# Half rows of 258 + 258 columns become 256 + 260 across a PSUM bank border, with rotating PSUM slots

## The chip, the cores and the metric

The kernel runs on 1 core of one Trainium2 chip. The metric is the device time of that core in microseconds (us). TensorE (PE) does the matrix products, VectorE (DVE) and ScalarE (ACT) the elementwise work, GpSimd (POOL) a little of it, and SyncE (SP) issues the transfers (DMA).

## The reference

One step of a decoder layer for a prompt of 1024 tokens and 8 sample tokens, so 1032 columns, with 1024 channels:

```python
shift, scale, gate = split(silu(c) @ w_ada + b_ada)
h = rms_norm(x, norm_g) * (1 + scale) + shift
(zq, zk, zv, zg_gla, zlr, zb, zc, zh, zg_sc, zx, zg_rg, zm) = split_cols(h @ w_in)
...
o, new_gla = gla_chunked(q, k, v, log_a, s_gla)      # 4 heads
y_gla = (rms_norm(o, gla_ng) * silu(zg_gla)) @ gla_wb
uc, new_sc = causal_dwconv(zc * zh, s_sc, sc_cw)
y_sc = (zb * uc * silu(zg_sc)) @ sc_wb
xc, new_rgc = causal_dwconv(zx, s_rgc, rg_cw)
hr, new_rgh = rg_lru(xc + rg_cb, ...)                # recurrence over tokens
y_rg = (hr * silu(zg_rg)) @ rg_wb
g1, g2, g3 = split(sigmoid(zm + b_merge))
out = (g1 * y_gla + g2 * y_sc + g3 * y_rg) @ w_out
return rms_norm(x + gate * out, final_gain), states
```

## The kernel before

Channels lie on the 128 partitions and tokens on the columns: a row of 1032 columns is two halves of 516 (`HW`). Every fp32 operand of the large products is split into a high and a low part (ACT writes the high part, DVE the rest), and a product is three matmuls: high x high, high x low, low x high. The program goes through four stages.

1. To about 130 us: the rows of x are loaded and normalised, and the modulation is computed from `w_ada`.
2. **The pair stage**, to about 1218 us: `h @ w_in` in 48 pairs of output tiles, in the order of `PAIRS`: for each of the 4 heads `qk`, `v`, `m`, `gg`, then 8 rounds of `rg`, `ch`, `m`, `bs`. A pair is computed with seven products instead of eight, in the order `SEQ = (1, 2, 6, 5, 7, 3, 4)`, from four sums and differences of the operand rows (`b1`, `b2`, `t12`, `t34`). A product is 24 matmuls: 4 slices of the contraction, 3 parts, 2 chunks of 258 columns (`CW`). The products of a pair collect in three PSUM slots: 1, 6, 7, 4 in slot c, 2 in slot b, 5 and 3 in slot d. So c is the first that a pair writes and the last that it leaves. After each product `post` reads the slot: ACT copies it to SBUF (`snap`), or DVE adds it to what was copied.
3. **The branch stage**, to about 1500 us: 24 products `proj`, 3 branches of 8 output tiles, each over 8 slices of the contraction with 3 parts and 3 chunks of 344 columns (`CH`): 72 matmuls. The operands are read back from DRAM (`ul`) and split into `uh` and `ul`. The gate's modulation (`ada_g`) is mixed in.
4. **The last stage**: `@ w_out` for three column ranges, the residual, the final norm.

A slot is a PSUM tile of two banks of 512 columns (`[P, 2, 512]`), and each chunk begins at the first column of its bank, so a half row in PSUM is two pieces of 258. There are three such slots. `slot_n` counts them off, so that each pair uses the same three in the same order: a pair's c lies where the c of the pair before lay. The weights of the pair stage pass through a ring of 3 raw tiles of 1024 columns (`wraw`) and 5 split half tiles (`wspl`). `zctx.close()` gives both pools back at the end of stage 2. Stages 3 and 4 open pools of their own there: `wpool` (2 raw, 3 high, 2 low tiles of 1024 columns) and `mmp` (2 PSUM tiles of three banks).

Independent small work is put between the matmuls: `fill` holds steps, and `tick` runs one after every fourth matmul in program order. A scheduler then sets the final order of each engine's instructions; each engine, and SP's queue of transfers, executes in that order. In a round of the pair stage `RG.steps` (`chunk`, six groups `rgg` of three matmuls, then `rec`) lies inside the `ch` pair.

Of the kernel before, what the change touches and what calls it, by code (L numbers as in the profile page):

```python
# [10 lines left out]
OP = mybir.AluOpType  # L11
# [10 lines left out]
CW = HW // 2  # L22
# [55 lines left out]
def build(tc, a):  # L78
    nc = tc.nc
    from contextlib import ExitStack  # L80
    with ExitStack() as ctx:
# [43 lines left out]
        def c2(t):  # L125
            return t.rearrange("p (c n) -> p c n", c=2)

        def pv(ps):
            return ps[:, :, :CW]

# [74 lines left out]
        def ada_mm(blk, t, ws, i=None, kk=None):  # L205
            pg = ada_st[blk]
            m = 9 if len(ws) == 1 else 20
            for kk in range(2) if kk is None else (kk,):
                k = 2 * t + kk
                for i_ in range(len(ws)) if i is None else (i,):  # L210
                    c = csl if m == 9 else (c20, c20h)[i_]
                    pe.matmul(pg[:m], c[:, k, :], ws[i_][:, kk * 512:(kk + 1) * 512],  # L212
                              start=(k == 0 and i_ == 0), stop=(k == KT - 1 and i_ == len(ws) - 1))
# [80 lines left out]
        def ada_first(blk, t):  # L294
# [3 lines left out]
            with ExitStack() as order:  # L298
# [8 lines left out]
                ada_mm(blk, t, ws)  # L307
# [20 lines left out]
        def group_rstd():  # L328
# [25 lines left out]
        class Pair:  # L354
            def __init__(self, fa, fb, name, use):
                self.fa, self.fb, self.name, self.use = fa, fb, name, use
                self.w = {}
# [20 lines left out]
            def snap(self, ps, name, scale=1.0):  # L378
                s = snap_tile(self.name + name)
                act.activation(c2(s), pv(ps), AF.Copy, scale=scale)  # L380
# [33 lines left out]
        def add_ps(dst, ps, s, scale=None):  # L414
            if scale is None:
                vec.tensor_add(c2(dst), pv(ps), c2(s))
            else:
                vec.scalar_tensor_tensor(c2(dst), pv(ps), scale, c2(s), op0=OP.mult, op1=OP.add)

        def silu_half(dst, src, view):  # L420
            act.activation(view(dst), src, AF.Sigmoid)
            vec.tensor_mul(view(dst), src, view(dst))

        def flat(t):
            return t
# [12 lines left out]
        def lr_mm(ps_of, k, i, start, stop):  # L438
            for n, x in enumerate(hop[i, k % 4]):
                for c in range(2):  # L440
                    pe.matmul(ps_of(c), first["w"][:, k * P:(k + 1) * P], x[:, c * CW:(c + 1) * CW],
# [4 lines left out]
        def first_mm(k):  # L446
            if k == 0:
# [3 lines left out]
                first_ps.append(slot("lr_ps"))  # L451
            lr_mm(lambda c: first_ps[0][:, c, :CW], k, 1, k == 0, False)
            lr_mm(lambda c: first_ps[0][:, c, :CW], k + 4, 2, False, k == 3)
# [20 lines left out]
        class Gates:  # L474
# [24 lines left out]
            def c21(self, ps):  # L499
                act.activation(c2(half(self.gb, 0)), pv(ps), AF.Sigmoid, bias=self.bias(1))  # L500
# [13 lines left out]
        def alpha_input(p0, pg):  # L514
            zst = tmp("zst", F32R)
            gp.memset(zst[64:128].bitcast(F32), 1.0)
            for lo, hi in ((0, 80), (96, 112)):
                act.activation(c2(half(zst, 0))[lo:hi], pv(p0)[lo:hi], AF.Copy)
                for c in range(2):
                    act.activation(c2(half(zst, 1))[lo:hi, c], pg[c][lo:hi, :CW], AF.Copy)  # L520
            vec.tensor_sub(c2(half(zst, 0))[32:64], pv(p0)[32:64], c2(half(zst, 0))[32:64].bitcast(F32))
            for c in range(2):
                o = c2(half(zst, 1))[32:64, c]
                vec.tensor_sub(o, pg[c][32:64, :CW], o.bitcast(F32))
# [6 lines left out]
        class QK:  # L531
# [16 lines left out]
            def c21(self, ps):  # L548
                act.activation(c2(half(self.hd["k"], 0)), pv(ps), AF.Copy)
# [805 lines left out]
```

## Time and profile before

| | before |
|---|---|
| median of 3 runs | 1629.8 us (1626.99 to 1632.26) |
| the profiled execution's own time | 1629.37 us |
| its span from first to last instruction | 1627.6 us |
| mean granted TensorE clock | 0.983 of full speed |
| PE busy | 1542.9 us (95%), 11594 matmuls |
| DVE busy | 1041.9 us (64%) |
| ACT busy | 733.4 us (45%) |

The profile is of one execution. The own time has 1.8 us more than the span, which lies around the first and the last instruction. A matmul's busy time holds its way through the array, and matmuls overlap, so PE is read here by the distance from one start to the next and by its named waits.

### The profile page before, as it was taken

Reading aid. Unit: us, or ns where it says so; the run is one execution under the profiler, and the core shown is the slowest. Engines: PE = TensorE matmul, PEld = TensorE weight load, DVE = VectorE, ACT = ScalarE, POOL = GpSimd, SP = SyncE. Lnnn points to the kernel's source line nnn. Section 1 sums busy time; section 2 is a strip of 40 time slices with the busy share of each in tenths; the row PEclk is TensorE's granted clock in tenths of the full one; section 3 lists DMA queues with packets and bytes.
Section 4 is the critical chain, followed back from the end, with each engine's and each line's share of the span. In section 5 each row is a group of like instructions: output and inputs, shape, how many; then the busy total and the mean of one; then the engine's idle time right before and its main releaser. Section 6 shows DMA issues by size and latency. Waiting matters only on the chain.

```text
span 1627.6 us, 27671 instructions
## 1 busy us (share of the span) xinstructions
PE 1542.9 (95%) x11594; PEld 1494.1 (92%) x11594; DVE 1041.9 (64%) x1673; ACT 733.4 (45%) x1163; POOL 31.6 (2%) x27
## 2 busy tenths in 40 slices
PE   4899999999999899999999999999997999999996
PEld 3489999999999899999999999999996999999996
DVE  7877587695877957666677667585755343434543
ACT  5556365473565645464444535454543221111332
POOL 3000000000000000000000000000000000000011
PEclk8799999999999999999999999999998999999998
DMA  9011412223232131212121211213135576661423
GB/s 361 16 62 41 146 53 107 79 79 134 78 104 82 66 121 40 91 57 95 66 94 57 78 66 69 92 40 107 41 132 195 207 274 237 218 208 53 143 79 92
DMA packets 58139, 177.45 MB, mean 109 GB/s; under 512 B 7166, under 2 KB 17822, under 8 KB 58014
## 3 DMA queue, kind: packets, MB, share of 16 engines
q1 hardware_dynamic: 58014, 175.68, 30.8%
q8 instruction: 91, 1.49, 0.4%
q14 instruction: 34, 0.28, 0.1%
HBM read 132.64 MB, written 43.02 MB: 108 GB/s over the span
## 4 chain that ended last, share of the span: by engine, by line
PE 49%; ACT 6%; DVE 5%; issue 3%; POOL 1%; DMA 1%; POOLq 0%; SPq 0%; DVEq 0%; ACTq 0%
PE y_ps L1108 17%; PE bs_c L347 6%; PE m_c L347 5%; PE rg_c L347 5%; PE bs_d L347 3%; PE m_d L347 2%; PE rg_d L347 2%; PE ch_c L347 2%; PE bs_b L347 1%; PE rg_b L347 1%; PE wo_ps L1210 1%; PE wo_pg L1210 1%; DVE a L936 1%; PE ch_b L347 1%; PE rgg L914 1%
## 5 line engine op out<-in xcount | busy, mean ns | idle before, releaser
L1108 PE MATMUL y_ps<-uh,y_h 128*128 128x344 f32 x576 | 124.1, 323 | 12.7 <-ACT y_h L164 12.7
L1108 PE MATMUL y_ps<-uh,y_l 128*128 128x344 f32 x576 | 124.5, 322 | 1.9 <-DVE y_l L165 1.9
L1108 PE MATMUL y_ps<-ul,y_h 128*128 128x344 f32 x576 | 124.1, 322 | 0.0
L1108 PEld LDWEIGHTS y_ps<-uh,y_h 128*128 128x128 f32 x576 | 97.6, 190 | 13.3 <-ACT y_h L164 12.9
L1158 DVE TENSOR_TENSOR gl<-y_ps,gl 128x1032 f32<-128x1032 f32 x24 | 29.6, 1232 | 117.4 <-PE y_ps L1108 117.2
L1108 PEld LDWEIGHTS y_ps<-uh,y_l 128*128 128x128 f32 x576 | 97.7, 190 | 4.6 <-DVE y_l L165 4.0
L1108 PEld LDWEIGHTS y_ps<-ul,y_h 128*128 128x128 f32 x576 | 97.9, 190 | 0.9
L164 ACT ACTIVATE y_h<-y_r 128x1024 fp32r<-128x1024 f32 x24 | 25.5, 1062 | 129.6 <-PE y_ps L1108 99.6
L1237 POOL TENSOR_TENSOR yt<-yt,frs 128x776 f32<-128x776 f32 x8 | 14.6, 1856 | 1515.5 <-DVE frs L1234 1515.5
L164 ACT ACTIVATE uh<-ul 128x1032 fp32r<-128x1032 f32 x24 | 25.1, 1062 | 35.5 <-DMA ul<-us 35.5
L165 DVE TENSOR_TENSOR ul<-ul,uh 128x1032 fp32r<-128x1032 f32 x24 | 29.1, 1227 | 17.5 <-ACT uh L164 17.4
L165 DVE TENSOR_TENSOR y_l<-y_r,y_h 128x1024 fp32r<-128x1024 f32 x24 | 29.2, 1216 | 15.0 <-PE ada L212 12.6
L1210 PE MATMUL wo_ps<-mlo,wo_h 128*128 128x388 f32 (+1 forms) x96 | 31.3, 326 | 0.0
L1210 PE MATMUL wo_ps<-mhi,wo_h 128*128 128x388 f32 (+1 forms) x96 | 30.9, 322 | 0.2 <-DVE yt L1217 0.2
L863 DVE SCALAR_TENSOR_TENSOR xc<-xp,pk,xc 128x1022 f32<-128x1022 f32 (+2 forms) x24 | 30.7, 1278 | 0.3
L1210 PE MATMUL wo_pg<-mlo,wo_h 128*128 128x388 f32 (+1 forms) x96 | 30.7, 320 | 0.0
L1210 PE MATMUL wo_ps<-mhi,wo_l 128*128 128x388 f32 (+1 forms) x96 | 30.7, 319 | 0.0
L1210 PE MATMUL wo_pg<-mhi,wo_l 128*128 128x388 f32 (+1 forms) x96 | 30.7, 319 | 0.0
L1210 PE MATMUL wo_pg<-mhi,wo_h 128*128 128x388 f32 (+1 forms) x96 | 30.6, 319 | 0.0
L1227 ACT ACTIVATE fsq<-yt 128x388 f32<-128x388 f32 (+1 forms) x21 | 10.2, 489 | 44.0 <-DVE yt L1222 28.4
L708 ACT ACTIVATE vt<-po 128x128 f32<-128x128 f32 x64 | 14.2, 276 | 33.2 <-PE po L706 33.2
L711 DVE SCALAR_TENSOR_TENSOR S<-S,eB,po 128x256 f32<-128x256 f32 x28 | 13.4, 478 | 23.0 <-ACT vt L708 22.8
(2826 smaller groups left out, 5198.6 us busy)
## 6 DMA issues: line engine op xcount, KB each, us to landing
ul<-us SPq DMA_DIRECT2D x24, 516.0 KB, 6.1
gl<-gs SPq DMA_DIRECT2D x24, 516.0 KB, 6.2
y_r<-wb SPq DMA_DIRECT2D x24, 512.0 KB, 4.1
pps<-gl SPq DMA_DIRECT2D x16, 516.0 KB, 3.5
p<-pps SPq DMA_DIRECT2D x16, 516.0 KB, 5.7
wada<-w_ada SPq DMA_DIRECT2D x16, 512.0 KB, 10.2
gs<-ga SPq DMA_DIRECT2D x12, 516.0 KB, 2.6
gs<-gb SPq DMA_DIRECT2D x12, 516.0 KB, 2.6
```

The costliest lines, as they stand in the source:

```text
L164: act.activation(hi, raw, AF.Copy)
L165: vec.tensor_sub(lo, raw, hi.bitcast(F32))
L347: pe.matmul(ps[:, c, :CW], m[:, k * P:(k + 1) * P], x[:, c * CW:(c + 1) * CW], start=(first and k == 0 and n == 0), stop=(last and k == 3 ...
L708: act.activation(hd["o"][d][:, gcols(g)], po[:, d * P:(d + 1) * P], AF.Copy)
L711: vec.scalar_tensor_tensor(Sn, S, s["eB"][:, gl:gl + 1], po[:, DV:2 * DV], op0=OP.mult, op1=OP.add)
L863: vec.scalar_tensor_tensor(hv(out)[:, :, s:TH], hv(src)[:, :, :TH - s], w(i), hv(out)[:, :, s:TH], op0=OP.mult, op1=OP.add)
L914: pe.matmul(ps, m[:, ws], x[:, cs], start=(ii == 0), stop=(ii == 2))
L936: vec.tensor_tensor_scan(a2[:, ts], aa[:, ts], a2[:, ts], a2[:, TH - 1:TH] if i else 0.0, op0=OP.mult, op1=OP.add)
L1108: pe.matmul(ps[:, c, :CH], m[:, ks], x[:, c * CH:(c + 1) * CH], start=(k == 0 and i == 0), stop=(k == KT - 1 and i == 2))
L1158: vec.tensor_mul(v3(g), psv(ps), v3(g))
L1210: pe.matmul(own(o), m[:, ks], view(x), start=(k == 0 and i == 0), stop=(k == KT - 1 and i == 2))
L1237: (gp if ci < 2 else vec).tensor_mul(y, y, rst_[:, :w].unsqueeze(1).to_broadcast([P, 2, w]))
```

## The change

The two chunks of a half row become 256 and 260 columns. A slot is one tile of 1024 columns; the chunks lie in its columns 256 to 512 and 512 to 772, so they meet at the bank border, and ACT and DVE read a half row as one run of 516 columns. A pair with number n takes c in slot n, b in slot n + 1 and d in slot n + 2 (modulo 3): its c lies where the pair before had b, its b where that had d, its d where that had c. The pools of the pair stage stay open. `proj` becomes a generator that does one half row after the other, 48 matmuls into one slot each, with DVE's multiplication after each half. Its weights and those of the last stage pass through the pair stage's ring, in halves of 512 columns, and the last stage uses the three slots in turn.

```diff
-CW = HW // 2
-        zctx = ExitStack()
-        wz_pool = zctx.enter_context(tc.tile_pool(name="wz_pool", bufs=2))
-        slot_pool = zctx.enter_context(tc.tile_pool(name="slot_pool", bufs=1, space=bass.MemoryType.PSUM))
+        wz_pool = ctx.enter_context(tc.tile_pool(name="wz_pool", bufs=2))
+        slot_pool = ctx.enter_context(tc.tile_pool(name="slot_pool", bufs=1, space=bass.MemoryType.PSUM))
...
-        slot_n = [0]
-
-        def slot(name):
-            i = slot_n[0] % 3
-            slot_n[0] += 1
-            return slot_pool.tile([P, 2, 512], F32, name=name, tag=f"slot{i}", bufs=1)
+        def slot(name, i):
+            return slot_pool.tile([P, 1024], F32, name=name, tag=f"slot{i % 3}", bufs=1)
...
-        def pv(ps):
-            return ps[:, :, :CW]
+        CHUNKS = ((0, 256), (256, HW))
+
+        def pv(ps, c=None):
+            a0, b0 = CHUNKS[c] if c is not None else (0, HW)
+            return ps[:, 256 + a0:256 + b0]
...
                     for c in range(2):
-                        pe.matmul(ps[:, c, :CW], m[:, k * P:(k + 1) * P], x[:, c * CW:(c + 1) * CW],
+                        pe.matmul(pv(ps, c), m[:, k * P:(k + 1) * P], x[:, slice(*CHUNKS[c])],
...
                 if i == 1:
-                    self.c = slot(self.name + "_c")
+                    self.c = slot(self.name + "_c", self.n)
                 elif i == 2:
-                    self.b = slot(self.name + "_b")
+                    self.b = slot(self.name + "_b", self.n + 1)
                 elif i == 5:
-                    self.d = slot(self.name + "_d")
+                    self.d = slot(self.name + "_d", self.n + 2)
...
-        zctx.close()
-        wpool = ctx.enter_context(tc.tile_pool(name="wpool", bufs=2))
-        mmp = ctx.enter_context(tc.tile_pool(name="mmp", bufs=2, space=bass.MemoryType.PSUM))
...
         def load_w(src, name, tag=None):
-            raw = wpool.tile([P, 1024], F32, name=name + "_r", tag="wraw", bufs=2)
+            raw = wraw(name)
             sp.dma_start(raw, src)
...
+            w = [wspl(f"{name}_{i}") for i in range(2)]
+            for i in range(2):
+                split(raw[:, i * 512:(i + 1) * 512], *w[i])
+            return [[w[i][x] for i in range(2)] for x in range(2)]
 
         def proj(src, xhi, xlo, name):
-            whi, wlo = load_w(src, name)
-            ps = mmt(name + "_ps")
-            for k in range(KT):
-                ks = slice(k * P, (k + 1) * P)
-                for i, (m, x) in enumerate(((whi, xhi[k]), (whi, xlo[k]), (wlo, xhi[k]))):
-                    for c in range(NC3):
-                        pe.matmul(ps[:, c, :CH], m[:, ks], x[:, c * CH:(c + 1) * CH],
-                                  start=(k == 0 and i == 0), stop=(k == KT - 1 and i == 2))
-                        tick()
-            return ps
+            w = load_w(src, name)
+            for h in range(2):
+                ps = next_slot(name + "_ps")
+                for k in range(KT):
+                    whi, wlo = (x[k // 4][:, k % 4 * P:(k % 4 + 1) * P] for x in w)
+                    for i, (m, x) in enumerate(((whi, xhi[k]), (whi, xlo[k]), (wlo, xhi[k]))):
+                        for c in range(2):
+                            pe.matmul(pv(ps, c), m, half(x, h)[:, slice(*CHUNKS[c])],
+                                      start=(k == 0 and i == 0), stop=(k == KT - 1 and i == 2))
+                            tick()
+                yield h, pv(ps)
...
-                ps = proj(a["wb"][br, j], [t[0] for t in u], [t[1] for t in u], f"y{br}_{j}")
                 g = tmp("gl")
                 sp.dma_start(g, gs[br][j])
-                vec.tensor_mul(v3(g), psv(ps), v3(g))
+                for h, y in proj(a["wb"][br, j], [t[0] for t in u], [t[1] for t in u], f"y{br}_{j}"):
+                    vec.tensor_mul(half(g, h), y, half(g, h))
...
-                ps = gpt("wo_pg") if f % 2 else mmt("wo_ps")[:, 0]
+                ps = next_slot("wo_ps")
```

The scheduler's order changes with it. The first place is PE's stream where the `m` pair of the second round (`m5`, after `ch1`) begins. Before, `m5` has done product 2 in b and begun product 5 in d when product 1 comes in c, with a wait for DVE:

```order
L347 MATMUL m_b<-b2h_597,m5w_l 128x258 x2
L347 MATMUL m_d<-t12h_356,m5w_h 128x258 [waits DVE_49,Activation_49]
L347 MATMUL m_d<-t12h_356,m5w_h 128x258
L347 MATMUL m_d<-t12l_357,m5w_h 128x258 x2
L347 MATMUL m_c<-b1h_348,m5w_h 128x258 [waits DVE_49]
L347 MATMUL m_c<-b1h_348,m5w_h 128x258
L347 MATMUL m_c<-b1l_349,m5w_h 128x258 x2
```

Now products 1 (24 matmuls in c) and 2 (24 in b) stand ahead, product 6 follows in c, and product 5 is the first to write d:

```order
L342 MATMUL m_b<-b2h_597,m5w_l 128x260
L342 MATMUL m_c<-t12h_356,m5w_h 128x256 [waits Activation_49]
L342 MATMUL m_c<-t12h_356,m5w_h 128x260
...
L342 MATMUL m_c<-t12h_601,m5w_l 128x256
L342 MATMUL m_c<-t12h_601,m5w_l 128x260
L342 MATMUL m_d<-t12h_356,m5w_h 128x256 [waits DVE_49]
L342 MATMUL m_d<-t12h_356,m5w_h 128x260
```

The wait for DVE's read of the `ch` pair's c moved from the pair's first product in c to product 5, 72 matmuls into the pair.

The second place is PE's stream at the end of the pair stage. Before, the first product `y_0` of the branch stage waits for all transfer queues, DVE and ACT at once, with `uh` and `ul` the two parts of its operand rows:

```order
L347 MATMUL bs_c<-t34h_605,bs7w_l 128x258 x2
L1108 MATMUL y_0_ps<-uh_0_13438,y_0_h 128x344 [waits DMAHW3_49,DMAHW4_49,DMAHW2_49,DMAHW5_49,DMAHW1_49,DMAHW6_49,DMAHW0_49,DMAHW7_49,DVE_49,Activation_49]
L1108 MATMUL y_0_ps<-uh_0_13438,y_0_h 128x344 x2
L1108 MATMUL y_0_ps<-ul_0_13439,y_0_h 128x344 x3
L1108 MATMUL y_0_ps<-uh_0_13438,y_0_l 128x344 [waits DVE_49]
```

Now matmuls of the gate's modulation (`ada`) follow the last pair at once, and `y_0` takes its operand rows one by one, each with a wait of its own:

```order
L342 MATMUL bs_c<-t34h_605,bs7w_l 128x260
L207 MATMUL ada<-ada_0_0_h,c_94 20x512
L207 MATMUL ada<-ada_0_0_l,c20h 20x512 [waits DVE_49]
L1098 MATMUL y_0_ps<-uh_0_13430,y_0_0_h 128x256 [waits PE_49,Activation_49]
L1098 MATMUL y_0_ps<-uh_0_13430,y_0_0_h 128x260
...
L1098 MATMUL y_0_ps<-uh_1_13436,y_0_0_h 128x256 [waits Activation_49]
...
L1098 MATMUL y_0_ps<-ul_1_13437,y_0_0_h 128x256 [waits DVE_49]
```

In SP's queue the weights of `y_0` (`y_0_r`) stood behind the last result of the pair stage (`zb`) before:

```order
L483 DMA gs_114<-gb 128x1032
L1145 DMA ul<-us_109 128x1032 x6
L998 DMA us_111<-zb 128x1032
L1145 DMA ul<-us_109 128x1032 x2
L1092 DMA y_0_r<-wb 128x1024
L1092 DMA ada_0_r<-w_ada 128x1024
```

They now stand ahead of it, and of the last two gates:

```order
L1079 DMA y_0_r<-wb 128x1024
L475 DMA gs_114<-ga 128x1032
L475 DMA gs_114<-gb 128x1032
L1079 DMA ada_0_r<-w_ada 128x1024
L1079 DMA ada_1_r<-w_ada 128x1024
L1079 DMA y_1_r<-wb 128x1024
L1135 DMA ul<-us_109 128x1032 x6
L991 DMA us_111<-zb 128x1032
```

The first weights of the branch stage moved from behind the pair stage's last transfer to ahead of its last pair's results.

## Rows read from the trace of the kernel before

**Rows 1.** The page: busy time by engine.

```profile
PE 1542.9 (95%) x11594; PEld 1494.1 (92%) x11594; DVE 1041.9 (64%) x1673; ACT 733.4 (45%) x1163; POOL 31.6 (2%) x27
```

**Rows 2.** Windows: stretch, length, busy time and instructions by engine, granted clock, DMA.

```profile
300.00:400.00 100.00, 100.00 (x833) 98.62 (x833) 74.76 (x129) 56.97 (x109) 0.00 (x0) 1.00 0.27 97
...
1400.00:1440.00 40.00, 40.00 (x256) 40.00 (x255) 12.46 (x11) 4.14 (x4) 0.00 (x0) 1.00 0.78 269
```

**Rows 3.** PE's waits: for whom, us in total, times, longest.

```profile
PE y_ps L1108 <- ACT y_h L164: 12.7, 1, 12.7
PE m_c L347 <- DVE ch L967: 11.1, 8, 1.5
...
PE ch_c L347 <- ACT ch1u L380: 1.2, 1, 1.2
...
PE m_c L347 <- ACT m4u L380: 1.0, 1, 1.0
```

**Rows 4.** Timeline, PE alone: starts in four stretches without other matmuls between.

```profile
1206.70 0.40 PE L347 MATMUL bs_d<-t12h,bs7w_h 128*128 128x258 f32 x2
...
1215.40 0.40 PE L347 MATMUL bs_c<-t34h,bs7w_h 128*128 128x258 f32 x2
...
1460.28 0.63 PE L1108 MATMUL y_ps<-ul,y_h 128*128 128x344 f32 x3
...
1469.73 0.48 PE L1108 MATMUL y_ps<-uh,y_h 128*128 128x344 f32 x2
...
1529.85 0.34 PE L1210 MATMUL wo_ps<-mhi,wo_h 128*128 128x388 f32 x1
...
1533.56 0.34 PE L1210 MATMUL wo_pg<-mhi,wo_h 128*128 128x388 f32 x1
...
1599.76 0.28 PE L1210 MATMUL wo_pg<-mlo,wo_h 128*128 128x256 f32 x1
...
1607.35 0.28 PE L1210 MATMUL wo_pg<-mhi,wo_l 128*128 128x256 f32 x1
```

**Rows 5.** Timeline of the second round's `ch` pair, all engines.

```profile
629.02 0.32 PE L914 MATMUL rgg<-xch,rgwl 128*128 128x344 f32 x1
...
629.94 1.28 ACT L926 ACT_TABLE_LOAD   x1
...
635.24 0.51 PE L347 MATMUL ch_c<-t34h,ch1w_h 128*128 128x258 f32 x2 [1.21 <-ACT ch1u L380]
```

**Rows 6.** Timeline where the `m` pair follows it.

```profile
644.40 0.40 PE L347 MATMUL ch_c<-t34h,ch1w_l 128*128 128x258 f32 x2
...
648.34 0.68 DVE L967 TENSOR_TENSOR ch<-ch_c,cc 128x516 f32<-128x516 f32 x1
...
649.08 0.51 PE L347 MATMUL m_c<-b1h,m5w_h 128*128 128x258 f32 x2 [1.51 <-DVE ch L967]
```

**Rows 7.** Timeline and windows at the end of the pair stage.

```profile
1218.05 0.40 PE L347 MATMUL bs_c<-t34h,bs7w_l 128*128 128x258 f32 x2
...
1218.99 4.86 ACT L164 ACTIVATE uh<-ul 128x1032 fp32r<-128x1032 f32 x5
...
1222.37 4.66 DVE L165 TENSOR_TENSOR ul<-ul,uh 128x1032 fp32r<-128x1032 f32 x4
...
1224.21 0.42 SPq L1092 DMA_DIRECT2D y_r<-wb  x1
...
1230.05 1.06 ACT L164 ACTIVATE y_h<-y_r 128x1024 fp32r<-128x1024 f32 x1 [0.22 <-DMA y_r<-wb]
...
1231.16 1.23 PE L1108 MATMUL y_ps<-uh,y_h 128*128 128x344 f32 x3 [12.71 <-ACT y_h L164]
...
1245.37 0.63 PE L1108 MATMUL y_ps<-uh,y_h 128*128 128x344 f32 x3
...
1218.40:1231.16 12.76, 0.05 (x1) 0.00 (x0) 10.44 (x11) 8.54 (x9) 0.00 (x0) 0.71 0.62 229
1231.16:1236.49 5.33, 5.33 (x19) 5.33 (x19) 3.66 (x3) 2.67 (x3) 0.00 (x0) 0.50 0.80 283
```

More of the change, by code (lines that the diff above doesn't have):

```diff
@@ L306, in ada_first @@
                     split(raw, *ws)
-                ada_mm(blk, t, ws)
+                ada_mm(blk, t, [(w[:, :512], w[:, 512:]) for w in ws])
         def ada_end(blk):
@@ L333, in group_rstd @@
             for s in range(2):
-                ps = slot("rs_ps")
+                ps = slot("rs_ps", s + 1)
                 for g in range(4):
-                    rs["p"] = pe.matmul(ps[:, g // 2, g % 2 * W8:(g % 2 + 1) * W8],
+                    rs["p"] = pe.matmul(ps[:, 512 + (g - 2) * W8:512 + (g - 1) * W8],
                                         rs["sk"][:, (4 * s + g) * P:(4 * s + g + 1) * P], r, start=True, stop=True).ins
-                act.activation(c2(half(rstd, s)), pv(ps), AF.Copy)
+                act.activation(half(rstd, s), ps[:, 512 - 2 * W8:512 + 2 * W8], AF.Copy)
         def product(ps, w, i, ks=range(4), first=True, last=True):
@@ L440, in lr_mm @@
                 for c in range(2):
-                    pe.matmul(ps_of(c), first["w"][:, k * P:(k + 1) * P], x[:, c * CW:(c + 1) * CW],
+                    pe.matmul(ps_of(c), first["w"][:, k * P:(k + 1) * P], x[:, slice(*CHUNKS[c])],
                               start=(start and n == 0), stop=(stop and n == 1))
@@ L548, in c21 @@
             def c21(self, ps):
-                act.activation(c2(half(self.hd["k"], 0)), pv(ps), AF.Copy)
+                act.activation(half(self.hd["k"], 0), pv(ps), AF.Copy)
         def alpha_steps(h):
@@ L639, in c21 @@
             def c21(self, ps):
-                act.activation(c2(half(self.hd["vt"][1], 0)), pv(ps), AF.Copy)
+                act.activation(half(self.hd["vt"][1], 0), pv(ps), AF.Copy)
         def v_steps(h):
@@ L966, in c21 @@
                 n, ch = self.n, self.ch
-                vec.tensor_mul(c2(half(ch, 0)), pv(ps), c2(half(self.cc, 0)))
+                vec.tensor_mul(half(ch, 0), pv(ps), half(self.cc, 0))
                 def cw(i):
@@ L1006, in build @@
             f, cls = where[kind]
-            pairs.append(Pair(*f(n), f"{kind}{n}", cls(n)))
+            pairs.append(Pair(len(pairs), *f(n), f"{kind}{n}", cls(n)))
         masks()
@@ L1074, in build, with next_slot @@
             sp.dma_start(a[name], t)
-        zctx.close()
-        wpool = ctx.enter_context(tc.tile_pool(name="wpool", bufs=2))
-        mmp = ctx.enter_context(tc.tile_pool(name="mmp", bufs=2, space=bass.MemoryType.PSUM))
-        def v3(t):
-            return t.rearrange("p (c n) -> p c n", c=NC3)
-        def psv(ps):
-            return ps[:, :, :CH]
-        def mmt(name):
-            return mmp.tile([P, NC3, 512], F32, name=name, tag="mm", bufs=2)
+        slot_n = [len(pairs)]
+        def next_slot(name):
+            slot_n[0] += 1
+            return slot(name, slot_n[0] - 1)
@@ L1090, in load_w @@
         def load_w(src, name, tag=None):
-            raw = wpool.tile([P, 1024], F32, name=name + "_r", tag="wraw", bufs=2)
+            raw = wraw(name)
             sp.dma_start(raw, src)
             if tag:
-                hi, lo = (bt(tag, name + x, F32R)[:, :1024] for x in ("_h", "_l"))
-            else:
-                hi = wpool.tile([P, 1024], F32R, name=name + "_h", tag="whi", bufs=3)
-                lo = wpool.tile([P, 1024], F32R, name=name + "_l", tag="wlo", bufs=2)
-            split(raw, hi, lo)
@@ L1099, in load_w @@
[L1099 to L1111 removed]
+                w = [bt(tag, name + x, F32R)[:, :1024] for x in ("_h", "_l")]
@@ new lines, in load_w @@
+                split(raw, *w)
+                return [[t[:, i * 512:(i + 1) * 512] for i in range(2)] for t in w]
+            w = [wspl(f"{name}_{i}") for i in range(2)]
+            for i in range(2):
+                split(raw[:, i * 512:(i + 1) * 512], *w[i])
+            return [[w[i][x] for i in range(2)] for x in range(2)]
+        def proj(src, xhi, xlo, name):
+            w = load_w(src, name)
[9 more added lines that the diff above has]
+                yield h, pv(ps)
@@ L1203, in build @@
             for f in range(8):
-                ps = gpt("wo_pg") if f % 2 else mmt("wo_ps")[:, 0]
+                ps = next_slot("wo_ps")
                 o = ps[:, :w]
-                whi, wlo = wo[f]
                 for k in range(KT):
-                    ks = slice(k * P, (k + 1) * P)
+                    whi, wlo = (x[k // 4][:, k % 4 * P:(k % 4 + 1) * P] for x in wo[f])
                     for i, (m, x) in enumerate(((whi, mhi[k]), (whi, mlo[k]), (wlo, mhi[k]))):
-                        pe.matmul(own(o), m[:, ks], view(x), start=(k == 0 and i == 0), stop=(k == KT - 1 and i == 2))
+                        pe.matmul(own(o), m, view(x), start=(k == 0 and i == 0), stop=(k == KT - 1 and i == 2))
                 if f % 2 == 0:
```

60 lines of the change are left out of this document (28 added, 32 removed).

## Prediction

> **What bounds the kernel now.** I read the page first: PE is busy for 95% of the span, DVE for 64% and ACT for 45% [rows 1]. So the time is PE's: the matmuls at their rate, plus the stretches in which PE waits. A window in the heads' part of the pair stage shows PE without a gap at full clock [rows 2]; there only a cheaper matmul can help. PE's waits come next [rows 3]. From the pair stage on, three kinds count: 12.7 us once, ahead of the first product of the branch stage; 11.1 us in 8 pieces, where an `m` pair needs slot c, from which DVE still reads the `ch` pair; and 1.2 us in each of 7 rounds (the row of `ch1u` stands for them), where the seventh product of a `ch` pair needs ACT's copy of the sixth. The first round has a few odd ones, the longest 1.0 us. The waits of the first 130 us belong to loading and normalising, which the change leaves alone. Third I read the distance between matmul starts, since 8064 matmuls of 258 columns make up the pair stage and 1728 of 344 the branch stage.
>
> **What a matmul costs.** Four stretches have nothing else between [rows 4]. Of 258 columns, 72 matmuls start in 8.70 us: 120.8 ns each. Of 344 columns, 60 (20 rows of 3) in 9.45 us: 157.5 ns. Of 388 columns, 21 in 3.71 us: 176.7 ns. Of 256 columns (two runs of 128), 64 in 7.59 us: 118.6 ns. The line through 256 and 344 rises by 0.442 ns a column, and gives 176.9 for 388, as measured. For 258 it gives 119.5, but 120.8 is measured, 1.3 ns more. The forms on the line read operand rows from a column that is a multiple of 4 (16 bytes). Of the two 258s the second starts at column 258, 8 bytes beside such a place. The new chunks start at 0, 256, 516 and 772, all multiples of 4. If that is the reason, two chunks cost 118.6 + 120.4 = 239.0 ns in place of 241.6, and the 4032 chunk pairs of the pair stage save 10.5 us. If the reason is another one, they save 0, since 516 columns stay 516 columns; no row lets me expect a loss. I take the alignment, because three forms lie on one line and the only one off it is the one that starts askew. I book 9 us of the 10.5, as in part of each `ch` pair PE follows ACT and not its own rate.
>
> Here the Trainium skill would say otherwise. Its page "TensorE: Matmul & The Clock Gate", section "Back-to-back issue gap", gives columns divided by 2.4 plus 2.5 ns at full clock, whatever the address; this makes, as an estimate, 110.0 ns for 258 columns, and 220.0 for the two chunks before and after alike. The trace's 120.8 lies above it; whether addresses play a part, no run here shows yet. By the rule the chunks would bring nothing.
>
> **The branch stage.** A product was 72 matmuls at 157.5, 11.34 us; now it is 96, or 48 chunk pairs at 239.0, 11.47 us. For the 23 products after the first that is 3.0 us more; at 241.6 it would be 5.9. I take 3. More DVE instructions (two multiplications of half rows, weights split in halves) lie under PE's work: the window 1400 to 1440 has DVE busy for 12.5 of 40 us [rows 2].
>
> **The `m` waits.** In round 2 the last matmuls of the `ch` pair's c start at 644.40, DVE's read begins at 648.34 and takes 0.68, and the `m` pair starts at 649.08 after 1.51 us of idling [rows 6]. DVE is thus some 4.4 us late. Before, PE bridged part of it with products 2 and 5. Now the new c is the old b, long read, and the first to write the old c is product 5. Ahead of it stand 72 matmuls of the pair, of which 6 come earlier than the last `ch` product: 66 at 119.5 ns cover 7.9 us. So the 11.1 us go. What is late next: DVE must after its read do about two full rows, two taps of full rows and the weights of product 5 before it splits those of product 7. At 0.68 us a half row [rows 6] and 1.17 a full one [rows 7] they are ready at about the time when PE gets there; I expect at most a few tenths of a us. The new b is the old d, whose read has product 4 and the new product 1, 48 matmuls or 5.7 us, to hide in.
>
> **The `ch` waits.** These stay. Between the end of the fourth `rgg` group (629.02) and PE's going on (635.24) lie 6.2 us of ACT: table loads, an exponential, two sigmoids, the copy [rows 5]. In PE's order 31 pair matmuls and 6 of `rgg` stood in between, 4.7 us; now 33 and 6 do, 4.9 us, and two fewer stand ahead of that group. That is 0.45 us a round, 3 us in seven rounds, not the 8.4 of the waits. Of the first round's odd waits I book 1 us.
>
> **The end of the pair stage.** PE's last pair matmul ends about 1218.4. The weights of `y_0` are issued only at 1224.21, split at 1230.05, and PE starts at 1231.16; the clock granted is 0.71 of full speed while PE idles and 0.50 in the 5.3 us after it [rows 7], the lower of its two levels, 1.2 GHz. The next product starts at 1245.37. So `y_0` takes 27.0 us, of which its matmuls need 11.3. Now no pool is closed, its weights are loaded and split before the last pair ends, and PE takes each operand row as it comes. DVE sets the pace. It has seven `ul` at 1.17 us [rows 7], one full row and one half for the last pair's result, and four halves of weights, at 0.68 each: 8.2 + 1.2 + 0.7 + 2.7 = 12.8 us, and about 2 us for ACT's part ahead of it. `y_0` should end some 15.5 us after the last pair, and PE will have done in that time 7 of the modulation's matmuls (1.6 us at 0.23 for 512 columns, by the line above) and about 12 of `y_1` (1.4 us). That saves 27.0 - 15.5 + 3.0 = 14.5 us. PE has little to do in the first 5 us, and the clock may fall again; 5.3 us at half speed would cost 2.65 us. I take 13, with bounds of 10 and 14.5.
>
> **The sum.** 11.1 + 3 + 1 + 9 + 13 - 3 = 34.1 us. The profiled execution's own time is 1629.4, its span 1627.6, its place in the middle of the runs (median 1629.8): 1629.4 - 34.1 = 1595.3, forecast 1595 us. Every addition to ACT, DVE and SP is booked at nothing, since PE is the engine that all others wait for. If DVE's cover were gone, the 48 half-row multiplications (0.68 for half of 1.2) would add some 4 us in the branch stage.
>
> **Rivals.**
> - *Only the columns count* (chance 0.24). For it: the excess is only 1.3 ns, and the 258s are the only form with two chunks. Against it: three widths on one line. The 9 us fall away and the branch stage costs 2.9 more: 1595 + 12 = 1607. The rule of the Trainium skill's page "TensorE: Matmul & The Clock Gate", above, gives this for the chunks.
> - *The gap moves into the splits* (0.10). DVE or the transfers (three weight tiles now go ahead of the six `ul`) come later than I add up, and the clock stays at 0.5 for longer; half of the 13 us is lost: 1601.
> - *The `m` wait comes back at product 7's weights* (0.07). Against it stands my sum of DVE's work, for it that it comes out even. Half of 11.1 us back: 1601.
> - *Slower: the branch stage waits for transfers* (0.03). Its DMA engines are busy for 0.78 at 269 GB/s while PE has no gap [rows 2], and SP issues in one order, in which a transfer that waits for a ring tile holds up all behind it. If PE lost more than 1.7 us in each of 23 products, 39 us, the kernel would be slower by over 0.3%; at 2 us it gives 1641. Against it: the ring has three raw tiles where `wpool` had two, and five half tiles where it had two full low ones, so the next weights are ahead by more.
>
> **How the numbers follow.** The forecast has 0.56. What a measurement can tell from no change is about 0.3%, 5 us. Faster takes the forecast and the first three rivals, less a little for mishaps that I have not seen: 0.93. Same: 0.04, a milder form of the last rival. Slower: 0.03. The range goes from 1583 (the full 10.5 and 14.5 us, and small waits that I have not booked) to 1608 (the first rival), and leaves out some 2 in 10.
>
> **What would show it.** PE's list of waits without `m_c <- DVE ch` and without `y_ps <- ACT`; `ch_c <- ACT` still there at about 1.0 in each of 7 rounds. Two chunks in 239 ns where no other matmul lies between; at 241 to 242 the first rival holds. `y_0` finished about 15 us after the last pair, and in the branch stage 48 chunk pairs in 11.5 us without waits. The forecast is wrong if PE waits at new places: product 5 or 7 of `m`, `ul` rows of `y_0`, or weights of the branch stage.

## The result and the profile after

| | before | after |
|---|---|---|
| median | 1630.3 us (1626.99 to 1632.26, 4 runs) | 1590.7 us (1590.05 to 1592.04, 4 runs) |
| the profiled execution's own time, span | 1629.37, 1627.6 us | 1590.05, 1588.2 us |
| forecast | | 1595 us (1583 to 1608) |

The ratio is 0.976, with an interval of 0.9743 to 0.9778: 39.6 us faster, where 34.1 had been worked out. The sum came out close, but several of its terms were off, in both directions. PE is now busy for 96% of the span (1524.0 us), with 12170 matmuls, 576 more than in [rows 1].

PE's list of waits of after, as [rows 3] (for whom, us in total, times, longest):

```profile
PE wo_ps L1199 <- DVE yt L1206: 3.5, 1, 3.5
...
PE m_d L342 <- DVE m4w_l L160: 2.7, 1, 2.7
...
PE rgg L907 <- ACT xch L159: 2.2, 8, 0.4
...
PE ch_c L342 <- ACT ch3u L375: 0.9, 1, 0.9
```

The two long rows of [rows 3], `y_ps <- ACT` and `m_c <- DVE ch`, are gone. `ch_c` stays, as forecast, at 0.8 to 0.9 in each of 7 rounds. Three rows of those shown are new or larger than before: `wo_ps` in the last stage, `m_d` in the first round, and `rgg`, eight times 0.3 on average. In the first head a wait of 1.7 us for DVE's `vs` is new as well.

Where the time came from is read by cutting both spans at the same places: at the end of the last pair, at the start of the eighth product of the branch stage (`y_7`), and at the start of the last stage. Windows of before, then of after (stretch, length, busy time and instructions of PE, PEld, DVE, ACT, POOL, granted clock, DMA share, GB/s):

```profile
1218.29:1327.78 109.49, 94.91 (x554) 87.83 (x553) 45.30 (x43) 35.05 (x36) 0.00 (x0) 0.94 0.58 208
1327.78:1520.73 192.95, 192.95 (x1227) 192.95 (x1225) 77.67 (x66) 34.74 (x33) 0.00 (x0) 1.00 0.54 187
1520.73:1627.55 106.82, 93.52 (x584) 91.59 (x582) 48.97 (x93) 34.34 (x58) 14.61 (x8) 0.95 0.32 100
```

```profile
1189.80:1282.39 92.59, 92.09 (x722) 88.01 (x720) 48.98 (x65) 35.01 (x49) 0.00 (x0) 1.00 0.74 273
1282.39:1476.63 194.24, 194.24 (x1635) 194.24 (x1634) 82.45 (x100) 38.72 (x51) 0.00 (x0) 1.00 0.51 172
1476.63:1588.16 111.53, 95.25 (x584) 93.11 (x582) 46.29 (x91) 33.60 (x57) 14.61 (x8) 0.94 0.29 91
```

Up to the end of the pair stage 1218.29 - 1189.80 = 28.5 us are won, in the next stretch 109.49 - 92.59 = 16.9; the 17 products that follow cost 1.3 more, the last stage 4.7 more. 28.5 + 16.9 - 1.3 - 4.7 = 39.4, the difference of the spans.

In the pair stage one round shows the pattern. PE's timeline, the first matmul of `rg5`, `ch5`, `m9`, `bs5` and `rg6`, of before and then of after:

```profile
952.61 0.28 PE L347 MATMUL rg_b<-b2h,rg5w_h 128*128 128x258 f32 x1
973.25 0.28 PE L347 MATMUL ch_b<-b2h,ch5w_h 128*128 128x258 f32 x1
995.50 0.28 PE L347 MATMUL m_b<-b2h,m9w_h 128*128 128x258 f32 x1
1020.58 0.28 PE L347 MATMUL bs_b<-b2h,bs5w_h 128*128 128x258 f32 x1
1041.13 0.28 PE L347 MATMUL rg_b<-b2h,rg6w_h 128*128 128x258 f32 x1
```

```profile
935.16 0.28 PE L342 MATMUL rg_c<-b1h,rg5w_h 128*128 128x256 f32 x1
955.16 0.28 PE L342 MATMUL ch_c<-b1h,ch5w_h 128*128 128x256 f32 x1
977.20 0.28 PE L342 MATMUL m_c<-b1h,m9w_h 128*128 128x256 f32 x1
1000.06 0.28 PE L342 MATMUL bs_c<-b1h,bs5w_h 128*128 128x256 f32 x1
1020.06 0.28 PE L342 MATMUL rg_c<-b1h,rg6w_h 128*128 128x256 f32 x1
```

The round goes from 88.52 to 84.90 us: `rg` wins 0.64, `ch` 0.21, `m` 2.22, `bs` 0.55. The terms of the sum for such a round were 1.4 for `m`, 0.45 for `ch`, and 0.75 for the chunks (9 us times 336 of 4032 pairs of chunks), 2.6 in all. So there is more in it than its named waits and the chunks, and `ch` gave least. (By the first starts the last product of `ch` is counted with `m`, in both kernels alike.)

### The profile page after: what moved, and what is told of

It reads as the page before. It is cut to its first block, busy times and chain, and to the rows that moved or that the text cites. A ratio compares the mean times of both kernels' runs of the same rounds, so it can differ in the third digit from the quotient of the medians.

```text
span 1588.2 us, 29025 instructions
## 1 busy us (share of the span) xinstructions
PE 1524.0 (96%) x12170; PEld 1485.4 (94%) x12170; DVE 1048.2 (66%) x1731; ACT 738.4 (46%) x1197; POOL 31.6 (2%) x27
## 4 chain that ended last, share of the span: by engine, by line
PE 73%; DVE 14%; issue 5%; ACT 5%; DMA 1%; POOL 1%; POOLq 0%; DVEq 0%; ACTq 0%; SPq 0%
PE y_ps L1098 17%; PE m_c L342 8%; PE bs_c L342 6%; PE m_d L342 4%; PE rg_c L342 3%; PE ch_c L342 3%; PE gg_c L342 3%; PE qk_c L342 3%; PE bs_d L342 3%; PE wo_ps L1199 3%; DVE xc L856 2%; PE qk_d L342 2%; PE ada L207 2%; PE rg_d L342 1%; PE m_b L342 1%
## 5 line engine op out<-in xcount | busy, mean ns | idle before, releaser
L1098 PE MATMUL y_ps<-ul,y_h 128*128 128x256 f32 (+1 forms) x768 | 153.8, 282 | 0.5 <-DVE ul L160 0.5
L1098 PE MATMUL y_ps<-uh,y_l 128*128 128x256 f32 (+1 forms) x768 | 153.9, 282 | 0.0
L1098 PE MATMUL y_ps<-uh,y_h 128*128 128x256 f32 (+1 forms) x768 | 153.7, 282 | 0.0
L1148 DVE TENSOR_TENSOR gl<-y_ps,gl 128x516 f32<-128x516 f32 x48 | 33.2, 694 | 65.7 <-PE y_ps L1098 64.7
L160 DVE TENSOR_TENSOR y_l<-y_r,y_h 128x512 fp32r<-128x512 f32 x48 | 32.9, 688 | 48.0 <-ACT y_h L159 43.9
L1199 PE MATMUL wo_ps<-mlo,wo_h 128*128 128x388 f32 (+1 forms) x192 | 62.7, 327 | 0.3 <-DVE mlo L160 0.3
L1199 PE MATMUL wo_ps<-mhi,wo_l 128*128 128x388 f32 (+1 forms) x192 | 62.0, 323 | 0.0
L1199 PEld LDWEIGHTS wo_ps<-mhi,wo_h 128*128 128x128 f32 x192 | 36.8, 192 | 3.9 <-DVE yt L1206 3.7
L1199 PEld LDWEIGHTS wo_ps<-mlo,wo_h 128*128 128x128 f32 x192 | 36.9, 192 | 0.9 <-DVE mlo L160 0.6
L1199 PEld LDWEIGHTS wo_ps<-mhi,wo_l 128*128 128x128 f32 x192 | 36.8, 192 | 0.3
```

The lines of the kernel that those rows point to most:

```text
L160: vec.tensor_sub(lo, raw, hi.bitcast(F32))
L1098: pe.matmul(pv(ps, c), m, half(x, h)[:, slice(*CHUNKS[c])], start=(k == 0 and i == 0), stop=(k == KT - 1 and i == 2))
L1148: vec.tensor_mul(half(g, h), y, half(g, h))
L1199: pe.matmul(own(o), m, view(x), start=(k == 0 and i == 0), stop=(k == KT - 1 and i == 2))
```

## The experiments

**The slots alone, and all but the slots.** `rotation_only` is the kernel before with the turned slots and nothing else; `slots_fixed` is the kernel after without them:

```
rotation_only:
-        slot_n = [0]
-
-        def slot(name):
-            i = slot_n[0] % 3
-            slot_n[0] += 1
-            return slot_pool.tile([P, 2, 512], F32, name=name, tag=f"slot{i}", bufs=1)
+        def slot(name, i):
+            return slot_pool.tile([P, 2, 512], F32, name=name, tag=f"slot{i % 3}", bufs=1)
...
-                    self.c = slot(self.name + "_c")
+                    self.c = slot(self.name + "_c", self.n)
slots_fixed:
-            pairs.append(Pair(len(pairs), *f(n), f"{kind}{n}", cls(n)))
+            pairs.append(Pair(0, *f(n), f"{kind}{n}", cls(n)))
```

> The kernel before with one part of the change alone: the slots are turned by one from pair to pair; chunks of 258 in a bank each and the old later stages stay. Theory (the parts add up): the m waits go, 11 us, and with the prediction's small terms 15 us, about 1615 us; with the pauses below 0.2 us in most other pairs (0.37 us in rg7) up to 1608. The ch waits stay at 0.8 to 1.2 us. Rival (DVE's lateness turns up one or two products later, at product 5 or at the weights of product 7): a wait of about 1 us in each m pair at a new place, 1626 to 1630 us.

> The changed kernel, but every pair takes slots 0, 1 and 2 as c, b and d again, so that product 1 of a pair writes the slot which the pair ahead still has to be read from. Theory (the slots are worth what the waits of the kernel before show): PE waits again for DVE's read of the ch pair at each m pair, 8 times about 1.4 us, 11 us; with the 4 us that the prediction booked for the ch waits and the first round this gives 15 us, about 1606 us. The trace of before also has pauses too short for the list of waits, some 0.1 us each where PE goes over to a product in c (0.37 us in the pair rg7, which the changed kernel does not have); if those are the slots' too, there are up to 47 such pairs and the time is nearer 1612. Rival (the waits went because of the chunks or the tail, not the turning): no m wait, 1591 us.

Measured: `rotation_only` 1612.6 us against 1628.0 of before on the same chip, ratio 0.9903 (0.9881 to 0.9925): 15.4 us. `slots_fixed` 1605.5, 14.7 us above the changed kernel. Both times lie in what the theory gave. In `slots_fixed` the waits of `m` for DVE's read come back with 6.7 us, less than the 11.1 of before; the rest lies in longer `ch` waits (1.3 a round) and in short pauses. In `rotation_only` no wait of `m` turned up at a new place in the rounds 2 to 8, so its rival falls. The same round of `rotation_only`:

```profile
943.62 0.28 PE L343 MATMUL rg_c<-b1h,rg5w_h 128*128 128x258 f32 x1
963.92 0.28 PE L343 MATMUL ch_c<-b1h,ch5w_h 128*128 128x258 f32 x1
985.96 0.28 PE L343 MATMUL m_c<-b1h,m9w_h 128*128 128x258 f32 x1
1009.14 0.28 PE L343 MATMUL bs_c<-b1h,bs5w_h 128*128 128x258 f32 x1
1029.45 0.28 PE L343 MATMUL rg_c<-b1h,rg6w_h 128*128 128x258 f32 x1
```

It takes 85.83 us, 2.69 less than before: `m` 1.90, and `rg`, `bs` and `ch` 0.34, 0.24 and 0.21, of which the list of waits had shown nothing for `rg` and `bs`. What such a pause is made of stands in the timeline of before: at the start of `rg7`, DVE reads slot c of `bs6`, and PE goes over to c a moment after.

```profile
1130.98 0.69 DVE L422 TENSOR_TENSOR sz<-bs_c,sz 128x516 f32<-128x516 f32 x1
...
1131.79 0.30 PEld L347 LDWEIGHTS rg_c<-b1h,rg7w_h 128*128 128x128 f32 x2 [0.15 <-issue]
```

DVE's read ends at 1131.67. The pause of 0.15 us before PE's weight load is put down to "issue" and is in no row of PE's list; `slots_fixed` has such pauses by name, `ch_c <- DVE sz`, 7 times, 0.2 us at most.

**The old tail.** The changed kernel's pair stage with the later stages of before (the diff is that of the change from the closing of the pools on, turned round).

> The changed kernel's pair stage, but the stages behind it as they were before: pools closed, three chunks of 344, weights in a pool of their own, five PSUM buffers in the last stage. Theory (the gap at the end of the pair stage belongs to the pools that are closed there): the wait of some 12.7 us for the weights of y_0 and the half clock behind it are back. By the prediction's terms 13 - 3 = 10 us more, 1601; by the places of the same products in both traces 15.6 us more until the last stage, which then runs some 5 us faster than now, so again about 10 to 11 us, 1601 us. Rival (the gap was the lateness of DVE and ACT in the old pair stage, which the turned slots have cured): less than 4 us of it come back, 1588 to 1592 us.

Measured: 1599.0 us, 8.3 above the changed kernel (by the ratios to before, 0.9825 and 0.976, 10.6). PE waits 12.8 us for `y_h` again, although the turned slots are there; the rival falls. `tail_old` and `rotation_only` (1612.6) ran in one session and differ only by the chunks of the pair stage, their cut and their place in PSUM: these are worth 13.6 us there.

**Five buffers in the last stage.** Before, this stage had four PSUM buffers, two large and two small ones (not five, as the expectations say); after the change it has three. Here it gets five.

```
-                ps = next_slot("wo_ps")
+                ps = gpt("wo_pg") if f % 2 else next_slot("wo_ps")
```

> The changed kernel with five PSUM buffers in the last stage again (the three slots for even products, the two small ones for odd), as the kernel before had them by another pool. Theory (with three slots PE runs into DVE in the third piece of the last stage): the new wait of 3.5 us goes and the matmuls around it close up, 3.5 to 5 us less than the changed kernel, about 1586 us. Rival (DVE itself ends last there): PE waits less, the end comes no sooner, 1590 us.

Measured: 1587.3 us (1582.5 to 1589.8), ratio to before 0.974 (0.9722 to 0.9758); against the 0.976 of the change alone the two intervals overlap. In the trace the wait for `yt` is gone, and the last stage takes 106.6 us, against 111.5 of after and 106.8 of before. The rows of after show what it was: DVE waits for a transfer of `x` at 1564.07, and with three slots PE has no place to go on to. Right behind the wait, from 1564.60 to 1568.30, the granted clock is 0.54 on average (its lower level, 1.2 GHz, for most of the time), which by that share costs another 1.7 us. The timeline, and the window of that stretch:

```profile
1564.07 0.89 DVE L1206 SCALAR_TENSOR_TENSOR yt<-wo_ps,modG,yt 128x256 f32<-128x256 f32 x2 [3.32 <-DMA yt<-x]
...
1564.61 0.56 PE L1199 MATMUL wo_ps<-mhi,wo_h 128*128 128x256 f32 x1 [3.47 <-DVE yt L1206]
```

```profile
1564.60:1568.30 3.70, 3.69 (x18) 3.69 (x19) 1.61 (x4) 2.66 (x6) 0.00 (x0) 0.54 0.20 54
```

**The exponential behind the sigmoids.**

```
-                    act.activation(self.gate[i][:, cs], ps, AF.Sigmoid, ...)
+                    self.last = act.activation(self.gate[i][:, cs], ps, AF.Sigmoid, ...).ins
...
+                with tc.issue_after(self.last):
                     act.activation(aa, r, AF.Exp, scale=nsp8[:, n:n + 1])
```

> The changed kernel with one order more on ACT: the exponential of a recurrence waits until the last of its six sigmoids has been issued. Now it lies between the fourth and the fifth, with a table load ahead of it and one behind it, 3.7 us in all, and PE waits behind it 0.8 us for the copy of product 6 in each of 7 ch pairs. Theory (this place of the exponential is what the ch waits come from): the copy comes 3 us sooner and the 7 waits go, 5 to 6 us less than the changed kernel, about 1585 us. Rival (ACT is late as a whole): the wait moves to the next copy or to the m pair's weights, 1588 to 1591 us.

> The changed kernel with both: the exponential behind the sixth sigmoid, and five PSUM buffers in the last stage. Theory: both gains add up, 5 to 6 and 3.5 to 5 us, about 1581 us. Rival: one of them is hidden by the other or by DVE, 1585 to 1591 us.

Measured: 1584.1 us (ratio 0.9722, 0.9709 to 0.9736), 6.6 below the changed kernel, and with the five buffers 1577.4 (0.9677, 0.966 to 0.9695), below both kernels. The gains come on top of each other (13.3 us together, 6.6 and 3.4 by themselves), and with `exp_last` as the base the five buffers show clear of the noise: the two intervals lie apart. ACT's timeline of the fifth `ch` pair, of after and then of `exp_last`:

```profile
966.05 1.28 ACT L919 ACT_TABLE_LOAD   x1
967.35 1.16 ACT L919 ACTIVATE aa<-rgt,nsp 128x1032 f32<-128x1032 f32 x1
968.52 1.28 ACT L908 ACT_TABLE_LOAD   x1
969.82 0.98 ACT L908 ACTIVATE rgt<-rgg,pk 128x344 f32<-128x344 f32 x2
970.69 0.60 ACT L375 ACTIVATE ch5u<-ch_c 128x516 f32<-128x516 f32 x1
```

```profile
965.05 0.53 ACT L908 ACTIVATE rgt<-rgg,pk 128x344 f32<-128x344 f32 x1
965.48 0.59 ACT L375 ACTIVATE ch5u<-ch_c 128x516 f32<-128x516 f32 x1
966.09 1.28 ACT L920 ACT_TABLE_LOAD   x1
```

In after, 3.7 us of table loads and exponential stand ahead of the last sigmoids and of the copy `ch5u`, for which PE waits. With the exponential behind them the copy comes 2.9 us sooner, counted from the start of ACT's copy `xch` in the same pair (960.62 in after, 958.28 here). One of the seven waits is left in the list, with 0.3 us. So the `ch` waits came from this order on ACT; with it one of the two table loads goes, 1.28 us of the 2.9.

**The chunks.** Four runs change only where the half row is cut; PSUM is shifted so that the cut stays at the bank border. `chunks_turned` multiplies the second chunk first.

```
-        CHUNKS = ((0, 256), (256, HW))
+        CHUNKS = ((0, 258), (258, HW))      (or 260, or 254)
-            return ps[:, 256 + a0:256 + b0]
+            return ps[:, 254 + a0:254 + b0]      (or 252, or 258)
```

> The changed kernel with chunks of 258 and 258 columns instead of 256 and 260; slots, tail and the contiguous half row that crosses the bank border at its chunk border stay. The second chunk then reads its operand from a column that is 2 beside a multiple of 4, and the first one's place in PSUM starts at 254. Theory (the place where an operand starts counts): two chunks go from 238 back to 241 ns or a little more; 4032 pairs of chunks in the pair stage and 1152 in the branch stage cost some 3 ns each more, 15 us, about 1605 us. Rival (only columns count): two chunks stay at 238 ns, 1591 us. If it comes out far above 1605, the place in PSUM costs something of its own.

> The changed kernel with chunks of 258 and 258 columns as in the run chunks_258 (1604.5 us, against 1590.7 of the changed kernel), but in each pair of chunks the second half is multiplied first: 258 to 516, then 0 to 258. Nothing else differs; the odd start at column 258 is read just as often. Theory B (what costs is a chunk that begins in the 16 bytes in which the one ahead has ended): the pair of chunks falls back to about 238 to 239 ns, as turn against old in the bench (238.1 against 243.6), and the time comes to 1591 to 1595 us. Theory A (a start beside a multiple of 4 columns has its own price, as the prediction put it): no change against chunks_258, 1604 us.

> The changed kernel with chunks of 260 and 256 columns, meeting at the bank border; the second chunk reads from column 260, a multiple of 4 but not of 16. Theory (the second chunk's start counts, and a multiple of 4 columns, 16 bytes, is enough): two chunks stay at 238 to 239 ns and the time at 1591 to 1594 us. Rival (256 is a special place, a multiple of 16 and more): two chunks take 241 to 242 ns as with 258, 1604 us.

> The changed kernel with chunks of 254 and 262 columns; the second one reads from column 254, 2 beside a multiple of 4, as with 258, and ends at the same place as ever. Theory (as for the run with 260): two chunks take 241 to 242 ns, 1604 us. Rival (the two widths count, unequal ones being cheaper than twice 258): 238 ns, 1591 us.

Measured: 1604.5 us with 258 (13.8 more than the changed kernel), 1601.4 with 258 turned, 1586.9 with 260, and 1740.0 with 254. The price is read from the pair `rg5` in each, 84 pairs of chunks with no other work between: from its first start to that of `ch5`. The lines of after and of `rotation_only` stand above; here are 258, turned, 260, 254:

```profile
941.18 0.28 PE L342 MATMUL rg_c<-b1h,rg5w_h 128*128 128x258 f32 x1
...
961.48 0.28 PE L342 MATMUL ch_c<-b1h,ch5w_h 128*128 128x258 f32 x1
```

```profile
943.83 0.28 PE L342 MATMUL rg_c<-b1h,rg5w_h 128*128 128x258 f32 x1
...
964.02 0.28 PE L342 MATMUL ch_c<-b1h,ch5w_h 128*128 128x258 f32 x1
```

```profile
935.04 0.28 PE L342 MATMUL rg_c<-b1h,rg5w_h 128*128 128x260 f32 x1
...
955.02 0.28 PE L342 MATMUL ch_c<-b1h,ch5w_h 128*128 128x260 f32 x1
```

```profile
1035.32 0.28 PE L342 MATMUL rg_c<-b1h,rg5w_h 128*128 128x254 f32 x1
...
1055.60 0.28 PE L342 MATMUL ch_c<-b1h,ch5w_h 128*128 128x254 f32 x1
```

Divided by 84, a pair of chunks takes 238.1 ns with the second chunk at 256, 237.9 at 260, but 241.7 at 258, 240.4 at 258 turned and 241.4 at 254. The columns are 516 each time, so the rival that only columns count falls. The order has a share: turning it takes 1.3 of the 3.6 ns away, so neither theory A (no change) nor theory B (back to 238 to 239) holds for the turned run. In the dear cuts the chunks' widths and the slot's first column in PSUM are beside a multiple of 4 too. The place in PSUM is not it, for `rotation_only`, with 258 columns from the start of each bank, takes 241.7 as well; start and width are told apart only by the bench below. The 1740 us of the run with 254 are not the price of its chunks: its instructions come in another order, PE waits at places where the other kernels have none or little (23.0 us for `ab`, 15.5 for `xch`, 12.5 for `vs`), and the mean granted clock is 0.962, in after 0.983.

**Two benches.** Extra stretches of 96 matmuls on one operand row, which show the cost by itself. Each bench ran once; stretches are compared within a run.

> The changed kernel with 8 extra stretches of 96 matmuls between the pair stage and the branch stage, whose sums nobody reads; each stretch goes 48 times over two chunks of one operand row, with the weights changing after each pair of chunks as in a product, and only the operand's start columns, the widths and the places in PSUM differ. old: 0 and 258, 258 columns each, start of a bank each. new: 0 and 256, 256 and 260 columns, meeting at a bank border. fit: 0 and 260, 258 each, as old in PSUM. bank: as new, but a bank each. both: 2 and 258, 258 each, as old in PSUM. odd: 1 and 257, 256 and 260 columns, as new in PSUM. put: 0 and 260, 258 each, but in PSUM from 254 and from 514. old once more as a control. Theory (an operand start that is not a multiple of 4 columns costs some 3 ns): old 241, new 238, fit 238, bank 238, both 244, odd 244, put 238 ns for two chunks. Rival 1 (only columns count): all alike. Rival 2 (the place in PSUM counts, above all the bank): bank and fit as old, 241, and put different from new.

> The changed kernel with 16 extra stretches of 96 matmuls between the pair stage and the branch stage, as in the bench before it; sums unread, PSUM slots now turned so that no stretch waits for the one ahead. zero, skew, two, four, slim, wide and odd read one chunk of the operand over and over (columns 0 to 258, 258 to 516, 2 to 260, 260 to 518, 0 to 256, 256 to 516, 1 to 257); bank, new, old, turn, fit, upold and upnew go over two: bank, new, old and fit as in the bench before, turn as old with the second chunk first, upold and upnew as old and new on the second half of a row (from column 516). In the bench before, old took 244, fit and put 238, both 240 and odd 244 ns for two chunks: so a chunk that starts beside a multiple of 4 does not cost the same everywhere. Theory A (each start has its own price): zero, four and slim near 118, skew near 123, two near 120, odd near 122 ns a matmul, and the pairs are sums of their singles. Theory B (what costs is the way from one chunk to the next, where the second starts in the 16 bytes in which the first ends): skew alone is as fast as zero, and only old, turn and upold are above 240. Rival (only columns count): 118 for 256 and 119 for 258, whatever the start.

Starts of some stretches of the second bench; from one to the next stretch are 48 pairs of chunks:

```profile
1189.10 0.28 PE L1098 MATMUL kzero<-t34h,bs7w_h 128*128 128x258 f32 x1
1200.56 0.28 PE L1098 MATMUL kskew<-t34h,bs7w_h 128*128 128x258 f32 x1
1211.97 0.28 PE L1098 MATMUL ktwo<-t34h,bs7w_h 128*128 128x258 f32 x1
...
1280.39 0.28 PE L1098 MATMUL knew<-t34h,bs7w_h 128*128 128x256 f32 x1
1291.70 0.28 PE L1098 MATMUL kold<-t34h,bs7w_h 128*128 128x258 f32 x1
1303.38 0.29 PE L1098 MATMUL kturn<-t34h,bs7w_h 128*128 128x258 f32 x1
1314.82 0.28 PE L1098 MATMUL kfit<-t34h,bs7w_h 128*128 128x258 f32 x1
1326.23 0.28 PE L1098 MATMUL kupold<-t34h,bs7w_h 128*128 128x258 f32 x1
```

`new` takes 235.6 ns for two chunks, `fit` 237.7, `old` 243.3: with twice 258 columns, a second start at 260 in place of 258 wins most of the difference, so the start counts where the widths are the same. But `skew`, which reads nothing but the askew chunk, is not slower than `zero` (237.7 against 238.8), and `turn` takes 238.3: neither a price of its own for each start (theory A) nor theory B holds for all of them. `odd`, 256 columns from column 1, takes 241.9, and `upold`, the cut of `old` in the other half of the row, 240.0. In the first bench `both`, whose two chunks both start askew, is below `old` (240 and 244), against the theory. `fit` and `put` of the first bench take 11.74 and 11.73 us: the place in PSUM costs nothing.

## Why the prediction was right, and where not

The undone parts cost 14.7 (slots), 13.8 (chunks) and 8.3 us (tail), 36.8 together; against the 1628.0 us of before in those runs the change as a whole gives 37.2. The changed kernel was timed in another session, with before at 1630.3; by the ratios to before of each session the parts are 16.3, 15.5 and 10.6, 42 against 39. So the parts add up within some 3 us, as the sum assumed.

That the total came out 5 us from the sum is in part luck. By stretches, with what was booked for each: 28.5 us won in the pair stage (24.1), 16.9 at its end (13 less some 0.8 for the dearer products in that stretch), 1.3 lost in the 17 products (2.2), 4.7 lost in the last stage (nothing). Two misses of over 4 us one way, and one the other way. By its steps:

- **The `m` waits (11.1 us): right**, and so is that DVE is not late next, at product 5 or 7, in rounds 2 to 8.
- **A term was missing, at about 1 us a round: pauses below the list.** The sum took PE's losses from the list of waits alone. `rg` and `bs` win 0.34 and 0.24 us a round by the slots, and `m` 0.5 more than its 1.4, where the list names nothing.
- **The `ch` waits (3 us): wrong in size.** The named wait fell from 1.2 to 0.8 a round, nearly the 0.45 that was booked, but the pair won only 0.21 with its cheaper matmuls included. The step that set 4.9 us of PE's work against 4.7 counted PE alone. The chain it waits for runs on DVE and ACT, from `xch` to the copy, and it was not shortened; a faster PE waits for it twice, 0.3 at `xch`, which is new, and 0.8 at the copy. `exp_last` shows what the wait hung on.
- **The first round (1 us): not won, and the clock took more.** From `rg0` to `rg1` after takes 96.4 us, before 94.4. But `wo_five`, with the same order on PE up to the last stage, takes 93.9, 0.5 less than before. The sum's terms for this round, 1 for the odd waits, 1.4 for `m` and 0.75 for the chunks, come to some 3. What is missing went into a new wait: PE needs low weights of `m4` at product 5, and DVE, which does the taps of `ch0` first, splits them late:

```profile
561.96 0.68 DVE L160 TENSOR_TENSOR m4w_l<-m4b_r,m4w_h 128x512 fp32r<-128x512 f32 x1
...
562.70 0.58 PE L342 MATMUL m_d<-t12h,m4w_l 128*128 128x256 f32 x1 [2.72 <-DVE m4w_l L160]
```

  In after the granted clock was besides at its lower level, 1.2 GHz, for some time from PE's idling on; in `wo_five`, with a wait of 2.6 us, it was not. Windows of the `m4` pair, from its first matmul to that of `bs0`, of after and then of `wo_five`:

```profile
546.65:575.64 28.99, 25.76 (x195) 25.35 (x193) 24.26 (x41) 14.37 (x22) 0.00 (x0) 0.88 0.17 60
```

```profile
546.62:573.07 26.45, 23.38 (x194) 22.97 (x193) 24.09 (x41) 14.37 (x22) 0.00 (x0) 1.00 0.18 66
```

  The 2.5 us between them are all that the two first rounds differ by. The rival in which the `m` wait comes back at the weights thus holds in one round of eight, at product 5 instead of 7; "at most a few tenths" was right in the other seven.
- **The chunks (9 us): right in which cuts are cheap, size too small.** 241.6 to 239.0 ns was forecast, 241.7 to 238.1 measured, and 13.6 us for the pair stage (`rotation_only` against `tail_old`). The line of [rows 4] put 260 columns and 256 at 239.0; they are 0.9 below it. That each askew start has its price, as the prediction put it, is not borne out: the order counts too, and the bench's askew chunk alone is not dear. The Trainium skill's page "TensorE: Matmul & The Clock Gate", section "Back-to-back issue gap", has the columns alone in its formula. By it all cuts would cost the same; these runs differ by up to 3.8 ns a pair of chunks, so here the measurement decides against it.
- **The end of the pair stage (13 us): too small, 16.9.** `y_0` itself came as forecast. DVE reads both halves of its sum from 1204.89 on, 15.1 us after the last pair, where 15.5 had been worked out:

```profile
1204.89 1.30 DVE L1148 TENSOR_TENSOR gl<-y_ps,gl 128x516 f32<-128x516 f32 x2 [1.52 <-PE y_ps L1098]
```

  The term that was mis-sized is the 1.5 us taken off for a clock that might fall: PE was busy for 92.09 of the 92.59 us, at a granted clock of 1.00 all through, the higher level, 2.4 GHz. And a term was missing: in before, PE waited 1.9 us for low weights of later products in this stretch, which is gone.

```profile
PE y_ps L1108 <- DVE y_l L165: 1.9, 4, 0.6
```

- **The branch stage (-3 us): right in kind**, -1.3 in the 17 products that can be compared, where 2.2 of the 3 had been booked. PE's list has no waits for transfers: the slower rival did not come about.
- **The last stage: not in the sum, -4.7 us.** The change took one of its four PSUM buffers away, and no step looked at that stage. The wait of 3.5 us and the 1.7 at the lower clock behind it cover the loss; in `wo_five` both are gone. That the measured gain is still 5 us above the sum is because pauses, chunks and the tail's start gave more than was booked.

## What to carry to other kernels

Read matmul starts, not only the list of waits: here a buffer that was freed just too late cost some 0.2 us at each use and stood in no row. When stages come to share one ring, count the buffers that each later stage had before. And where a wait hangs on another engine's chain, making the waiting engine faster won next to nothing here; reordering the chain did.

## What the runs showed of the hardware that was not expected

With 516 columns in two matmuls, a cut at 256 or 260 takes 238.1 or 237.9 ns, one at 254 or 258 takes 241.4 or 241.7, and one at 258 with the second chunk first 240.4. In a stretch that goes over one row again and again the price of `turn`, 238.3, is the sum of those of its single chunks (119.4 and 118.9), but that of `old`, the same chunks the other way round, is not (243.3). Why is open: no run here separates the reading of the operand from the loading of weights beside it. The same columns at other places of PSUM, 0 and 512 or 254 and 514, took the same time.
